# A gated short convolution beside a long one: the gate's product leaves PSUM early, and the long convolution's steps get lower rates

## The chip, the cores and the metric

The kernel runs on one core of a Trainium2 chip. The metric is the device time of one execution in microseconds (us), as the median of several runs. One core has a matrix engine (TensorE, PE in the profile), a vector engine (VectorE, DVE), an activation engine (ScalarE, ACT), a general engine (GpSimd, POOL) and DMA queues (SP). TensorE writes its products to PSUM banks; the other engines read them from there.

## What is computed

One inference step of a two-layer encoder over 1088 columns (1024 of a new stream and 64 of a running one), 1024 channels wide. The change lies in layer 1, whose mixer runs a long gated convolution C and a short gated convolution D from one normalised input:

```python
def odd_mixer(h, hist_c, hist_d, w_in, w_out, c_conv_w, c_conv_b, c_ln_g, c_ln_b, d_conv_w):
    z = h @ w_in
    c_in = z[..., :C_WIDTH] * jax.nn.sigmoid(z[..., C_WIDTH:2 * C_WIDTH])
    c_ext = jnp.concatenate([hist_c.astype(z.dtype), c_in], axis=1)
    c = causal_dwconv(c_ext, c_conv_w) + c_conv_b            # width 31
    c = jax.nn.silu(layer_norm(c, c_ln_g, c_ln_b))
    o = 2 * C_WIDTH
    gate_b = z[..., o:o + D_WIDTH]
    gate_c = z[..., o + D_WIDTH:o + 2 * D_WIDTH]
    xt = z[..., o + 2 * D_WIDTH:]
    d_ext = jnp.concatenate([hist_d.astype(z.dtype), gate_c * xt], axis=1)
    d = gate_b * causal_dwconv(d_ext, d_conv_w)              # width 3
    y = jnp.concatenate([c, d], axis=-1) @ w_out
    return y, c_ext[:, -(C_KERNEL - 1):], d_ext[:, -(D_KERNEL - 1):]
```

`rms_norm` comes before it and a feed-forward block with squared ReLU after it; both layers have that block, and it takes most of the time.

## The kernel before

Data lie with channels on the 128 partitions and the columns along the free axis. Each operand of a matrix product is kept as a high and a low part (`split`: the activation engine makes the high part, line 176, the vector engine the low part, line 177), and each product is three matmuls (`mm3`, lines 268 to 270).

In layer 1 the 512 channels of each of C and D are four groups j of 128. Every projection of a group (`project`) is made in two halves of 544 columns, the right one (c=1) first. A half is a PSUM pair of two banks that takes 48 matmuls. There are two such pairs (`open_psum("m1", 2)`), used in turn, so TensorE can start a half only when the vector engine has emptied the pair of the half before the last. Three more banks (`psum3`) hold the running sum of the long convolution.

First come the projections of C, two for each group (`cg`, `ca`, in `conv_pairs`). Its width-31 convolution is 31 steps for each group. Those of groups 1 and 3 and the last 13 of group 2 run on the vector engine, each as one multiply-and-add over 1118 columns in PSUM (`on_vec`, line 1131; the last step of a group is line 1137, and in group 2 line 1142 adds GpSimd's part). That makes 75 steps, of which the first of each group is made by the activation engine (line 1110). Group 0 and the first 18 steps of group 2 run as a multiply on the activation engine (line 1118) and an add on GpSimd (line 1120).

These steps are not emitted group after group. They wait in two lists, and `some(rates)` takes from them after each half: the rate is added to a credit, and each whole unit of it takes one step. A step for GpSimd is tied behind the last instruction of the activation engine that was emitted before it (`issue_after`). Behind the 75 steps the vector list holds 21 steps of C's layer norm (`ln_steps`: sums on GpSimd, `centre` with a matmul on line 1209, `scale` with one on line 1222, `finish_`), in three chunks of columns.

Then `short_conv(j)` runs for each group. It makes three projections: `dc`, whose halves leave PSUM into a buffer `wide` (line 1158); `dx`, whose halves are multiplied with that buffer into `z` (line 1162); and `db`, the gate. Between `dx` and `db` the width-3 convolution makes `o` from `z` (the activation engine on line 1171, the vector engine twice on line 1173, for a piece of 1024 and one of 64 columns). For a half of `db` the vector engine multiplies `o` by the norm's factor (line 1180) and then by the PSUM pair (line 1181), which only then is free, and `split` makes `dd`.

After that comes the output product of D (key `o1d`): sixteen halves of 24 matmuls, each added to `x` on line 766. Then that of C (`o1c`), first for all of the left half of the columns, which needs the first two chunks of the layer norm.

The order of the instructions on an engine is not the order of the text. A list planner in the language puts every traced instruction in order by its own costs, and an instruction that stands later in the text may be put ahead of one that is not yet ready. On the chip each engine then runs its list in order.

Of the kernel before, what the change touches and what calls it, by code (L numbers as in the profile page):

```python
# [13 lines left out]
AF = mybir.ActivationFunctionType  # L14
ALU = mybir.AluOpType
# [5 lines left out]
T = SEQ + DEC  # L21
# [5 lines left out]
NH = 2 * NQ  # L27
C4 = [(NQ * i, NQ * i + NQ) for i in range(4)]
CW = 512
HB, HC, HD = 15, 30, 2  # L30
# [13 lines left out]
def segs(a, b, halo):  # L44

    out = []
    if a < SEQ:
        e = min(b, SEQ)
        out.append((0, halo + a, e - a))
    if b > SEQ:  # L50
        s = max(a, SEQ)
        out.append((s - a, 2 * halo + s, b - s))
    return out
# [3 lines left out]
def encoder(ctx, tc, ins, outs):  # L57
    nc = tc.nc
    act, dve, gp, pe, dma = nc.scalar, nc.vector, nc.gpsimd, nc.tensor, nc.sync
# [30 lines left out]
    def sb(shape, dt, tag, bufs):  # L90
        uid[0] += 1
        p = opened["right"][1] if tag in RIGHT else opened["left"][1] if tag in LEFT else pool
        return p.tile(shape, dt, tag=tag, bufs=bufs, name=f"{tag}_{uid[0]}")
# [48 lines left out]
    def xs(n=T, dt=F32):  # L142
        return sb([P, n], dt, "X", 8)
# [27 lines left out]
    def col(o):  # L171
        return par[:, o : o + 1]


    def split(hi, lo, src):
        act.activation(hi, src, AF.Copy)  # L176
        dve.tensor_tensor(lo, src, hi.bitcast(F32), ALU.subtract)  # L177
# [76 lines left out]
    def take(key, depth=4):  # L254
        while key not in made:
            n = len(made)
            ahead(sum(s for s, _ in made.values()) + 2)
            assert len(made) > n, key
        got = made.pop(key)[1]
        ahead(depth)  # L260
        return got
# [69 lines left out]
    def halves(t):  # L331
        return t.rearrange("p (h t) -> p h t", h=2)
# [416 lines left out]
    def add_out(m, c, w, t, ks):  # L749
        a = c * NH  # L750
        ps = pair()
        for i in range(2):
            mm3(
                ps[:, i, :NQ],
                [
                    (
                        w[0][:, q * P : (q + 1) * P],
                        w[1][:, q * P : (q + 1) * P],
                        t(0, k, c, i),
                        t(1, k, c, i),  # L760
                    )
                    for q, k in ks
                ],
            )
        xm = halves(x[m][:, a : a + NH])
        dve.tensor_tensor(xm, xm, ps[:, :, :NQ], ALU.add)
# [220 lines left out]


    h = h1
    RP, RD, NP2 = (2.85, 1.65), (2.4, 1.65), 18  # L990
    NC = 2 * HC + T
    ND = 2 * HD + T
    NO = HC + T
# [6 lines left out]
    dd = [tuple(sb([P, T], F32R, "dd", 8) for _ in range(2)) for _ in range(4)]  # L1000
    wide = lambda: sb([P, NH], F32, "wide", 5)
# [7 lines left out]
    def last_on_act():  # L1009
        return next(i for i in reversed(nc.cur_bb.bb.instructions) if i.engine == mybir.EngineType.Activation)  # L1010

    def some(*rates):
        for i, q in enumerate((on_dve, on_pool)):
            credit[i] += rates[i]
            while credit[i] >= 1:
                credit[i] -= 1
                if q:
                    with tc.issue_after(last_on_act()) if q is on_pool else nullcontext():
                        q.pop(0)()

    def r_of(c):
        return halves(acc[:, c * NH : c * NH + NH])
# [3 lines left out]
    def project(key, ps_of, rates):  # L1026

        w = take(key)
        for c in (1, 0):
            ps = pair()  # L1030
            for i in range(2):
                a = i * NQ
                mm3(
                    ps[:, i, :NQ],
                    [
                        (
                            w[0][:, k * P : (k + 1) * P],
                            w[1][:, k * P : (k + 1) * P],
                            h[c][0][k][:, a : a + NQ],
                            h[c][1][k][:, a : a + NQ],  # L1040
                        )
                        for k in MS
                    ],
                )
            if unnormed:
                assert unnormed.pop(0) == c
                rms_half(c, wide(), psum3().rearrange("p (h t) -> p h t", h=3)[:, :2])
                rr = halves(r2[:, c * NH : c * NH + NH])
                dve.tensor_tensor(rr, r_of(c), r_of(c), ALU.mult)
            ps_of(c, ps[:, :, :NQ])  # L1050
            some(*rates)

    def pieces(c, t, ps, g, halo):

        g = halves(g)
        if c == 0:
            return [(halves(t[:, halo : halo + NH]), ps, g)]
        out = []
        for i in range(2):
            for s, o, n in segs(NH + i * NQ, NH + i * NQ + NQ, halo):  # L1060
                out.append((t[:, o : o + n], ps[:, i, s : s + n], g[:, i, s : s + n]))
        return out
# [87 lines left out]
    def short_conv(j):  # L1150
        gc = [None] * 2
        z, o = xs(ND), xs()
        dve.memset(z[:, :HD], 0.0)
        dma.dma_start(out=z[:, HD + SEQ : 2 * HD + SEQ], in_=ins["sdT"][j])

        def gate_c(c, ps):
            gc[c] = wide()
            dve.tensor_tensor(halves(gc[c]), ps, halves(r2[:, c * NH : c * NH + NH]), ALU.mult)

        def gate_x(c, ps):  # L1160
            for o_, p, g in pieces(c, z, ps, gc[c], HD):
                dve.tensor_tensor(o_, p, g, ALU.mult)

        project(("dc", j), gate_c, RD)
        project(("dx", j), gate_x, RD)
        dma.dma_start(out=outs["cd_p"][j], in_=z[:, SEQ : SEQ + HD])
        dma.dma_start(out=outs["cd_s"][j], in_=z[:, ND - HD :])
        wk = lambda k: col(O_DW + 3 * j + k)
        for s, e, n in segs(0, T, HD):
            e -= HD  # L1170
            act.activation(o[:, s : s + n], z[:, e : e + n], AF.Copy, scale=wk(0))
            for k in (1, 2):
                dve.scalar_tensor_tensor(  # L1173
                    out=o[:, s : s + n], in0=z[:, e + k : e + k + n], scalar=wk(k), in1=o[:, s : s + n],
                    op0=ALU.mult, op1=ALU.add,
                )
        def gate_b(c, ps):
            a = c * NH
            oc = o[:, a : a + NH]
            dve.tensor_tensor(halves(oc), halves(oc), r_of(c), ALU.mult)  # L1180
            dve.tensor_tensor(halves(oc), halves(oc), ps, ALU.mult)  # L1181
            split(dd[j][0][:, a : a + NH], dd[j][1][:, a : a + NH], oc)

        project(("db", j), gate_b, RD)

    means = {}
# [50 lines left out]
    for j in range(4):  # L1237
        short_conv(j)
# [4 lines left out]
    for m in MS:  # L1243
        w = take(("o1d", m))
        for c in range(2):
            add_out(m, c, w, dh, [(k, k) for k in range(4)])
            some(1.5, 0)
    while on_dve or on_pool:
        some(1, 1)
    open_psum("f1", 4)  # L1250
# [133 lines left out]
```

## Time and profile before

| | us |
|---|---|
| median of 3 runs | 2098.84 (2098.55 to 2103.15) |
| the profiled execution's own time | 2099.91 |
| its span in the profile | 2098.1 |

The profiled execution is 1.07 us above the median. Its span leaves 1.8 us around it. Times in the rows are microseconds from the span's start unless marked ns; "x48" is a number of instructions; a bracket at the end of a row says how long the engine stood idle before it and whose end let it go on.

### The profile page before, as it was taken

Reading aid. Unit: us, or ns where it says so; the run is one execution under the profiler, and the core shown is the slowest. Engines: PE = TensorE matmul, PEld = TensorE weight load, DVE = VectorE, ACT = ScalarE, POOL = GpSimd, SP = SyncE. Lnnn points to the kernel's source line nnn. Section 1 sums busy time; section 2 is a strip of 40 time slices with the busy share of each in tenths; the row PEclk is TensorE's granted clock in tenths of the full one; section 3 lists DMA queues with packets and bytes.
Section 4 is the critical chain, followed back from the end, with each engine's and each line's share of the span. In section 5 each row is a group of like instructions: output and inputs, shape, how many; then the busy total and the mean of one; then the engine's idle time right before and its main releaser. Section 6 shows DMA issues by size and latency. Waiting matters only on the chain.

```text
span 2098.1 us, 38092 instructions
## 1 busy us (share of the span) xinstructions
PE 2006.6 (96%) x15212; PEld 1974.7 (94%) x15212; DVE 1630.4 (78%) x2697; ACT 948.0 (45%) x1710; POOL 261.7 (12%) x172
## 2 busy tenths in 40 slices
PE   7999989999998999998999999989999999999995
PEld 5799989999998999998999999989999999999994
DVE  7884787676779888878499967897676779888867
ACT  6233554444445444445453425654344455444443
POOL 5200220000000000002276730210000000000003
PEclk9999999999999999999999999999999999999997
DMA  4223213434348444422211132223434366545402
GB/s 153 73 62 104 81 65 142 162 126 162 127 155 264 149 136 152 137 83 100 74 42 41 41 70 87 91 78 137 152 135 153 134 215 198 153 134 154 131 32 85
DMA packets 120434, 250.36 MB, mean 119 GB/s; under 512 B 16384, under 2 KB 31360, under 8 KB 116160
## 3 DMA queue, kind: packets, MB, share of 16 engines
q1 hardware_dynamic: 120256, 247.93, 36.3%
q8 instruction: 119, 1.95, 0.4%
q14 instruction: 59, 0.48, 0.1%
HBM read 176.26 MB, written 71.63 MB: 118 GB/s over the span
## 4 chain that ended last, share of the span: by engine, by line
PE 74%; DVE 17%; issue 2%; ACT 2%; POOL 2%; DMA 2%; DVEq 0%; SPq 0%; ACTq 0%; POOLq 0%
PE pp L861 20%; PE pp L863 20%; PE pp L862 19%; DVE ps L1131 4%; PE pp L268 3%; PE pp L269 3%; PE pp L270 3%; PE ps L268 2%; PE ps L269 2%; PE ps L270 2%; DVE Q L177 1%; DVE Wl L177 1%; DVE W L177 1%; DVE X L940 1%; DVE X L1173 1%
## 5 line engine op out<-in xcount | busy, mean ns | idle before, releaser
L861 PE MATMUL pp<-FA,W 128*128 128x272 f32 x1792 | 522.7, 293 | 36.5 <-DVE X L940 25.9
L861 PE MATMUL pp<-Q,W 128*128 128x272 f32 x1792 | 518.7, 290 | 2.0 <-DVE Q L903 1.1
L863 PE MATMUL pp<-FA,W 128*128 128x272 f32 x1792 | 520.1, 290 | 0.0
L862 PE MATMUL pp<-FA,W 128*128 128x272 f32 x1792 | 519.0, 290 | 0.0
L862 PE MATMUL pp<-Q,W 128*128 128x272 f32 x1792 | 516.9, 289 | 1.0 <-DVE Q L177 1.0
L863 PE MATMUL pp<-Q,W 128*128 128x272 f32 x1792 | 517.1, 289 | 0.0
L861 PEld LDWEIGHTS pp<-FA,W 128*128 128x128 f32 x1792 | 340.1, 190 | 43.2 <-DVE X L940 30.5
L862 PEld LDWEIGHTS pp<-FA,W 128*128 128x128 f32 x1792 | 342.7, 191 | 0.2
L862 PEld LDWEIGHTS pp<-Q,W 128*128 128x128 f32 x1792 | 340.3, 190 | 1.5 <-DVE Q L177 1.4
L861 PEld LDWEIGHTS pp<-Q,W 128*128 128x128 f32 x1792 | 338.9, 189 | 2.9 <-DVE X L940 1.4
L863 PEld LDWEIGHTS pp<-FA,W 128*128 128x128 f32 x1792 | 341.0, 190 | 0.0
L863 PEld LDWEIGHTS pp<-Q,W 128*128 128x128 f32 x1792 | 339.1, 189 | 0.0
L176 ACT ACTIVATE W<-RAW 128x512 fp32r<-128x512 f32 (+3 forms) x308 | 182.4, 595 | 150.5 <-PE pp L863 108.5
L177 DVE TENSOR_TENSOR W<-RAW,W 128x512 fp32r<-128x512 f32 (+3 forms) x308 | 204.7, 666 | 56.5 <-ACT W L176 55.7
L268 PE MATMUL pp<-Q,Wl 128*128 128x272 f32 x768 | 226.1, 294 | 12.8 <-DVE X L1181 10.4
L940 DVE TENSOR_TENSOR X<-X,pp 128x544 f32<-128x544 f32 (+1 forms) x280 | 191.7, 691 | 57.1 <-PE pp L863 54.4
L269 PE MATMUL pp<-Q,Wh 128*128 128x272 f32 x768 | 224.7, 293 | 0.0
L270 PE MATMUL pp<-Q,Wh 128*128 128x272 f32 x768 | 224.0, 292 | 0.0
L950 POOL TENSOR_TENSOR acc<-acc,sq 128x544 f32<-128x544 f32 (+1 forms) x24 | 29.7, 1236 | 1345.4 <-ACT sq L949 1344.8
L176 ACT ACTIVATE W<-e 128x512 fp32r<-128x512 f32 (+3 forms) x210 | 124.6, 593 | 158.6 <-PE pp L863 127.4
L177 DVE TENSOR_TENSOR W<-e,W 128x512 fp32r<-128x512 f32 (+3 forms) x210 | 136.9, 652 | 66.5 <-ACT W L176 66.2
L268 PEld LDWEIGHTS pp<-Q,Wl 128*128 128x128 f32 x768 | 147.9, 193 | 14.6 <-DVE X L1181 11.0
(220 smaller groups left out, 3541.7 us busy)
## 6 DMA issues: line engine op xcount, KB each, us to landing
RAW<-in_wf SPq DMA_DIRECT2D x58, 1024.0 KB, 5.2
vr<-hd SPq DMA_DIRECT2D x119, 272.0 KB, 2.8
hd<-Q SPq DMA_DIRECT2D x112, 272.0 KB, 2.3
Q<-hd SPq DMA_DIRECT2D x105, 272.0 KB, 2.8
hd<-vr SPq DMA_DIRECT2D x98, 272.0 KB, 2.2
raw<-in_wi SPq DMA_DIRECT2D x18, 512.0 KB, 3.4
X<-in_xT SPq DMA_DIRECT2D x8, 544.0 KB, 4.1
xd<-X SPq DMA_DIRECT2D x8, 544.0 KB, 2.7
```

Of the source, the lines that this page charges most:

```text
L176: act.activation(hi, src, AF.Copy)
L177: dve.tensor_tensor(lo, src, hi.bitcast(F32), ALU.subtract)
L268: pe.matmul(ps, ll, rh, start=s, stop=False)
L269: pe.matmul(ps, lh, rl, start=False, stop=False)
L270: pe.matmul(ps, lh, rh, start=False, stop=e)
L861: pe.matmul(ps, ll, hi, start=bool(s), stop=False, skip_group_check=True)
L862: pe.matmul(ps, lh, lo, start=False, stop=False, skip_group_check=True)
L863: pe.matmul(ps, lh, hi, start=False, stop=e, skip_group_check=True)
L940: dve.tensor_tensor(t, t, ps, ALU.subtract if f in (1, 4, 6) else ALU.add)
L950: (dve if j == 3 else gp).tensor_tensor(at, at, sq, ALU.add)
L1131: return dve.scalar_tensor_tensor(out=o, in0=z[:, k : k + NO], scalar=wk(k), in1=o, op0=ALU.mult, op1=ALU.add)
L1173: dve.scalar_tensor_tensor(out=o[:, s : s + n], in0=z[:, e + k : e + k + n], scalar=wk(k), in1=o[:, s : s + n], op0=ALU.mult, op1=ALU.add,)
```

## The change

The gate's half is multiplied by the norm's factor out of PSUM into a `wide` buffer, and the pair is free after that one instruction. The width-3 convolution is emitted after the first half's instruction. After the second half's, both halves of `o` are multiplied by their buffers, the right one first, and split. The vector rate in D's stage goes from 2.4 to 1.9 steps for each half, and in the output product of D from 1.5 to 2.

```diff
-    RP, RD, NP2 = (2.85, 1.65), (2.4, 1.65), 18
+    RP, RD, NP2 = (2.85, 1.65), (1.9, 1.65), 18
...
-        for s, e, n in segs(0, T, HD):
-            e -= HD
-            act.activation(o[:, s : s + n], z[:, e : e + n], AF.Copy, scale=wk(0))
-            for k in (1, 2):
-                dve.scalar_tensor_tensor(
-                    out=o[:, s : s + n], in0=z[:, e + k : e + k + n], scalar=wk(k), in1=o[:, s : s + n],
-                    op0=ALU.mult, op1=ALU.add,
-                )
+
+        def convolve():
+            for s, e, n in segs(0, T, HD):
+                e -= HD
+                act.activation(o[:, s : s + n], z[:, e : e + n], AF.Copy, scale=wk(0))
+                for k in (1, 2):
+                    dve.scalar_tensor_tensor(
+                        out=o[:, s : s + n], in0=z[:, e + k : e + k + n], scalar=wk(k), in1=o[:, s : s + n],
+                        op0=ALU.mult, op1=ALU.add,
+                    )
+
+        gb = {}
+
         def gate_b(c, ps):
-            a = c * NH
-            oc = o[:, a : a + NH]
-            dve.tensor_tensor(halves(oc), halves(oc), r_of(c), ALU.mult)
-            dve.tensor_tensor(halves(oc), halves(oc), ps, ALU.mult)
-            split(dd[j][0][:, a : a + NH], dd[j][1][:, a : a + NH], oc)
+
+            gb[c] = wide()
+            dve.tensor_tensor(halves(gb[c]), ps, r_of(c), ALU.mult)
+            if c == 1:
+                return convolve()
+            for i in (1, 0):
+                a = i * NH
+                oc = o[:, a : a + NH]
+                dve.tensor_tensor(oc, oc, gb[i], ALU.mult)
+                split(dd[j][0][:, a : a + NH], dd[j][1][:, a : a + NH], oc)
...
             add_out(m, c, w, dh, [(k, k) for k in range(4)])
-            some(1.5, 0)
+            some(2, 0)
```

## Rows read from the trace of the kernel before

**Rows 1.** The page: busy time, share of the span and instructions of each engine.
```profile
PE 2006.6 (96%) x15212; PEld 1974.7 (94%) x15212; DVE 1630.4 (78%) x2697; ACT 948.0 (45%) x1710; POOL 261.7 (12%) x172
```

**Rows 2.** The waits of TensorE, 1100 to 1265 us: total, times, longest.
```profile
PE pp L268 <- DVE X L1181: 10.4, 3, 4.3
```

**Rows 3.** Windows: length, busy time of each engine, granted clock, DMA share, GB/s.
```profile
1109.30:1231.30 122.00, 110.58 (x823) 109.02 (x822) 115.37 (x111) 48.87 (x49) 77.43 (x31) 0.94 0.13 36
1231.30:1261.30 30.00, 30.00 (x241) 30.00 (x240) 11.36 (x18) 4.36 (x7) 6.34 (x7) 1.00 0.56 137
1261.30:1315.20 53.90, 52.70 (x399) 50.52 (x398) 40.97 (x84) 30.66 (x58) 0.00 (x0) 1.00 0.20 66
```

**Rows 4.** The timeline of TensorE in D's stage: start, duration, instruction, idle before.
```profile
1110.07 0.39 PE L268 MATMUL pp<-Q,Wl 128*128 128x272 f32 x1 [0.17 <-DVE wide L1158]
...
1138.14 0.39 PE L268 MATMUL pp<-Q,Wl 128*128 128x272 f32 x1 [3.02 <-DVE X L1181]
...
1222.25 0.60 PE L268 MATMUL pp<-Q,Wl 128*128 128x272 f32 x1 [4.35 <-DVE X L1181]
```

**Rows 5.** The timeline of VectorE in D's stage: start, duration, instruction, idle before.
```profile
1114.30 1.39 DVE L1131 SCALAR_TENSOR_TENSOR ps<-cin,par,ps 128x1118 f32<-128x1118 f32 x1 [1.36 <-ACT ps L1110]
...
1128.08 0.71 DVE L1162 TENSOR_TENSOR X<-pp,wide 128x544 f32<-128x544 f32 x1
...
1137.37 0.71 DVE L1181 TENSOR_TENSOR X<-X,pp 128x544 f32<-128x544 f32 x1
...
1228.84 1.23 DVE L1142 TENSOR_TENSOR cin<-cin,X 128x1024 f32<-128x1024 f32 x1 [1.44 <-POOL X L1120]
...
1231.28 0.72 DVE L1158 TENSOR_TENSOR wide<-pp,r 128x544 f32<-128x544 f32 x1
1237.29 0.72 DVE L1158 TENSOR_TENSOR wide<-pp,r 128x544 f32<-128x544 f32 x1 [5.29 <-PE pp L270]
...
1261.34 0.72 DVE L1181 TENSOR_TENSOR X<-X,pp 128x544 f32<-128x544 f32 x1 [3.84 <-PE pp L270]
```

**Rows 6.** Groups of VectorE by form, 1109 to 1232 us: count, busy us, mean ns.
```profile
L1131 DVE SCALAR_TENSOR_TENSOR ps<-cin,par,ps 128x1118 f32<-128x1118 f32 x42 | 57.9, 1380 | 1.8 <-ACT ps L1110 1.4
L177 DVE TENSOR_TENSOR Wl<-raw,Wh 128x1024 fp32r<-128x1024 f32 x9 | 18.2, 2021 | 0.0
L1173 DVE SCALAR_TENSOR_TENSOR X<-X,par,X 128x1024 f32<-128x1024 f32 x6 | 9.8, 1629 | 0.0
L1173 DVE SCALAR_TENSOR_TENSOR X<-X,par,X 128x64 f32<-128x64 f32 x6 | 7.4, 1238 | 0.0
L177 DVE TENSOR_TENSOR dd<-X,dd 128x544 fp32r<-128x544 f32 x6 | 5.6, 939 | 0.7 <-ACT dd L176 0.7
L1158 DVE TENSOR_TENSOR wide<-pp,r 128x544 f32<-128x544 f32 x7 | 5.0, 720 | 2.5 <-PE pp L270 2.5
L1181 DVE TENSOR_TENSOR X<-X,pp 128x544 f32<-128x544 f32 x6 | 4.3, 714 | 0.0
L1180 DVE TENSOR_TENSOR X<-X,acc 128x544 f32<-128x544 f32 x6 | 4.1, 716 | 0.0
```

**Rows 7.** The timeline of GpSimd: the first adds after one of its pauses.
```profile
1140.05 11.90 POOL L1120 TENSOR_TENSOR X<-X,X 128x1118 f32<-128x1118 f32 x4 [14.75 <-ACT X L1118]
```

**Rows 8.** The timeline of VectorE at moments when GpSimd pauses: three two-input instructions.
```profile
1126.59 0.27 DVE L1173 SCALAR_TENSOR_TENSOR X<-X,par,X 128x64 f32<-128x64 f32 x1
...
1131.13 1.27 DVE L1173 SCALAR_TENSOR_TENSOR X<-X,par,X 128x1024 f32<-128x1024 f32 x1
...
1224.19 1.22 DVE L177 TENSOR_TENSOR Wl<-raw,Wh 128x1024 fp32r<-128x1024 f32 x1
```

**Rows 9.** The timeline from the layer norm's first matmul to D's last output half.
```profile
1261.14 0.77 PE L1209 MATMUL ps<-t,onec 128*128 128x364 f32 x2
...
1292.42 1.12 DVE L177 TENSOR_TENSOR Q<-cin,Q 128x180 fp32r<-128x180 f32 x4
...
1315.18 0.72 DVE L766 TENSOR_TENSOR X<-X,pp 128x544 f32<-128x544 f32 x1 [2.29 <-PE pp L270]
```

## The prediction

> **What bounds the kernel now.** I read the page first: TensorE is busy for 96% of the span, VectorE for 78% [rows 1], so the kernel is TensorE's except where something starves it. The waits of TensorE in D's stage name one cause: three waits, 10.4 us, for line 1181, the instruction that frees the gate's PSUM pair [rows 2]. The reader should see in the windows that from 1109.3 to 1231.3 VectorE works 115.4 of 122.0 us while TensorE's granted clock averages 0.94, and that in the next 30 us VectorE works only 11.4 and TensorE never stops [rows 3]. So the work of VectorE is crowded into the first three groups and missing in the fourth.
>
> What TensorE loses follows from its pace. In the fourth group four halves leave PSUM in 1261.34 - 1237.29 = 24.05 us, 6.01 for each pair [rows 5]. From 1110.07, where the third half of the stage starts [rows 4], to 1261.34, where the last one is complete [rows 5], lie 22 pairs, 132.3 us at that pace; it took 151.3. The loss is **19.0 us**, and no change inside this stage can give more. Of it 10.4 are the waits on line 1181, and the clock, partly at its lower level of 1.2 GHz, costs (1 - 0.94) x 122 = 7.3. The rest is short waits.
>
> How late line 1181 is: the second half of `dx` is taken at 1128.08, and the first half of the gate only at 1137.37, 9.3 us later [rows 5]. In between stand a weight split, conv steps, the width-3 convolution and two multiplications by the norm's factor.
>
> **The change part by part.**
>
> *The gate's product.* Before, a half of the gate costs two multiplications, 0.716 from SBUF alone and 0.714 with PSUM; after, one from PSUM into a buffer, for which line 1158 with the same operands stands at 0.720, and one from SBUF alone, 0.716 as line 1180 [rows 6]. The work is the same; what changes is that the pair is free after the first of the two, and the convolution and its products no longer stand before it. The three waits, 3.02 and 4.35 among them [rows 4], go. Behind the waiting instruction on VectorE stood conv steps, which nobody was waiting for. The buffers: four of five `wide` tiles are in use in a group, so I price this wait at nothing; a half's lateness, 6.0, is the price if one were missing. The state's two DMAs stay where they were, ahead of the convolution.
>
> *But is the waiting replaced by VectorE's own load?* From the first eviction of the first group to that of the fourth, VectorE has 115.4 us of work [rows 3], TensorE 18 pairs, 18 x 6.01 = 108.2. VectorE is the slower one. A reordering alone leaves 115.4 to be done before the fourth group. Of its 6.6 us of idleness there, 1.36 (a group's first step on the activation engine) and 1.44 (GpSimd's part of group 2) stay [rows 5]; the rest is mostly waiting for a TensorE that had itself been held (2.5 before line 1158 [rows 6]) and goes.
>
> *The lower rates.* At 2.4, 18 halves of this stage after the 22.8 steps of C's stage make 66 of the 75 conv steps due by 1231. Yet all 75 are done there: 42 of line 1131 lie in that stretch [rows 6], line 1142, which ends the last group, is at 1228.84 [rows 5]. So the steps run nine ahead of what the rates ask, that is, they fill any gap in which nothing of earlier text is ready. A rate that is not the limit can be lowered without moving anything: at 1.9 they would merely be 18 ahead. I take zero. If the rate did bind, nine of the steps would leave the stretch, 9 x 1.38 = 12.4 us [rows 6].
>
> *GpSimd against VectorE.* Instructions of VectorE with two SBUF inputs are sometimes much longer: the 64-column piece of line 1173 takes 0.27 and the 1024-column piece 1.27 when GpSimd pauses, a weight split 1.22 [rows 8]; in the stretch the means are 1.238, 1.629 and 2.021 [rows 6], while line 1131, with one input in PSUM, has a mean of 1.380 [rows 6] and 1.39 in the row shown [rows 5]. The excess is 6 x 0.97 + 6 x 0.36 + 9 x 0.80 + 6 x 0.22 (the split of `dd`, 0.939 against 0.72) = 16.5 us. Line 1180 has none, since GpSimd stands still there: 14.75 us, because its next multiply is tied behind the split of `dd` [rows 7]. After, it is tied behind the width-3 convolution and starts sooner, so the new products and the four free 1024-column pieces can be held. Below, this is worth down to -16.5 (nothing held any more); above, ten instructions at the 0.97 of the worst group, +9.7. I take the nearest rows in size: 6 x 0.22 as for `dd`, 4 x 0.36 as for the group's mean, **+2.7**, because the number of GpSimd's adds is unchanged and what meets one here no longer meets it elsewhere.
>
> The Trainium skill, SBUF — State Buffer, section "Who interferes with whom", says that such a VectorE instruction and a GpSimd one that reads SBUF exclude each other for the whole of the instruction. The lengthening in the rows agrees. Taken by itself it speaks against this change, and the second rival below is what it would do.
>
> *The sum.* The fourth group's first eviction: 1109.3 + 115.4 + 2.8 + 2.7 = 1230.2, against 1231.28 [rows 5]. But before, TensorE then had five pairs to do, as it had been stopped before it could fill the second; now it stands with both full, and four remain after the 0.72 of the eviction: 1230.2 + 0.72 + 24.05 = 1255.0 against 1261.34, **6.4 gained**. At the end the second half of `dd` in the fourth group comes after one product more than before: 0.7 lost, for the output product waits for it. The layer norm's steps fall due later, but TensorE has 53.9 us there (next part); zero. The remaining kernel shifts. So 5.7 us: 2099.91 - 5.7 = 2094.2 on the profiled execution, and, since that one is 1.07 above the median, **2093** for the median. What a measurement of this kernel tells from no change is 0.3%, 6.3 us; the forecast lies just inside it.
>
> **The rivals.**
>
> *The rates bind after all.* Then VectorE has 115.4 - 12.4 = 103.0 against 108.2, TensorE never waits, and the whole 19.0 less 0.7 comes back; the moved steps fit into the 18.6 idle microseconds of the fourth group [rows 3]. 2099.91 - 18.3 - 1.07 = 2080.5. Against it stand the nine steps ahead. Chance 0.20.
>
> *GpSimd's hold eats it.* With +9.7 for +2.7 the sum becomes -1.3 (gain 5.7 - 7.0), that is 2100 for the median. For it: the pause at line 1180 that goes [rows 7]. Against: GpSimd's 77.4 us [rows 3] are not more than before. Chance 0.13. This is also the case of a change that does what it says and shows nothing.
>
> *The norm becomes late.* The side of slower. With 1.9 and 2 the norm's first matmul (step 79 of the list) is due in the sixth half of D's output product, (79 - 68.4) / 2 = 5.3, not at its start; half a pair each, 3.0 us, makes it 18 us later. From that matmul to the last split that the left half of C's output product needs, 1261.14 to 1293.54, it takes 32.4; 18 + 32.4 = 50.4, and D's output product lasts 1315.18 - 1261.34 = 53.8 [rows 9]. So 3.4 are to spare, and each microsecond more is paid on TensorE. It decides from a slip of 3.4 + 5.7 + 6.3 = 15.4 us, if the norm's steps, now in between sixteen evictions, take half as long again; for that price, 8 to 10 us lost, the median would be 2107. Chance 0.07.
>
> **How the numbers follow.** The forecast case has 0.60, with its own range 2089 to 2097: 0.27 of it lies beyond 0.3% faster, 0.33 within. With the first rival (0.20 faster), the second (0.11 same, 0.02 slower) and the third (0.06 slower, 0.01 same): faster 0.47, same 0.45, slower 0.08. The range is 2081 to 2100: the first rival's neighbourhood and the second's, without the third.
>
> **What would show it.** Right: no wait of TensorE on the gate's product above 1 us; instead short waits spread over the evictions, at full clock; VectorE still over 95% busy until the fourth group; the last conv step still before the fourth group's first eviction; that eviction within 2 us of 1230, and D's output product starting about 6 us earlier. Wrong: conv steps in the fourth group or in D's output product (first rival); line 1173 or the products at 2 us and more throughout (second); TensorE waiting at the start of C's output product (third). What most endangers the forecast is the claim that the order ignores the rates: with it falls the size, not the sign.

## The result, and the profile after

| | before | after |
|---|---|---|
| median of 5 runs, us | 2101.61 | 2087.64 |
| ratio, 95% interval | 1 | 0.9948 (0.9936 to 0.9960) |
| the profiled execution's span, us | 2098.1 | 2085.8 |

The kernel became 0.5% faster: about 11 us, with an interval of 8 to 13, where 5.7 had been forecast. The median before had been 2098.84 in the three runs shown ahead of the prediction and is 2101.61 in these five, so the ratio, and not the difference of the two medians, is the size to use.

The windows of the same three stretches: D's first three groups, the fourth group, D's output product (columns as in [rows 3]).

```profile
1110.08:1226.20 116.12, 110.28 (x861) 108.25 (x861) 109.80 (x110) 48.69 (x49) 78.34 (x30) 1.00 0.13 37
1226.20:1251.47 25.27, 25.27 (x204) 25.27 (x203) 12.62 (x19) 4.37 (x7) 8.36 (x8) 1.00 0.67 165
1251.47:1303.57 52.10, 52.10 (x398) 50.51 (x397) 42.13 (x84) 30.45 (x56) 0.00 (x0) 1.00 0.21 67
```

The first stretch fell from 122.0 to 116.1 us, the second from 30.0 to 25.3, the third from 53.9 to 52.1; that is 12.4 of the span's 12.3. The granted clock of the first stretch is 1.00, where it was 0.94: TensorE ran at 2.4 GHz throughout. VectorE works 109.8 us in it instead of 115.4, with as many instructions within one or two.

The waits of TensorE, 1090 to 1330 us (total, times, longest), against [rows 2]:

```profile
PE pp L268 <- DVE X L1162: 3.6, 3, 1.4
PE pp L268 <- DVE wide L1185: 2.0, 2, 1.5
PE pp L268 <- DVE wide L1158: 0.2, 1, 0.2
```

Line 1185 is the gate's new eviction (the instruction that empties the PSUM pair). What had been three waits of 3 to 4.3 us on one instruction are six of 1.5 us at most, on all three evictions: TensorE still waits for VectorE, by less.

The timeline of VectorE, to be read against [rows 5]:

```profile
1134.40 0.71 DVE L1185 TENSOR_TENSOR wide<-pp,acc 128x544 f32<-128x544 f32 x1
...
1188.40 2.81 DVE L1131 SCALAR_TENSOR_TENSOR ps<-cin,par,ps 128x1118 f32<-128x1118 f32 x2 [2.20 <-ACT ps L1110]
...
1224.86 1.22 DVE L1142 TENSOR_TENSOR cin<-cin,X 128x1024 f32<-128x1024 f32 x1 [1.46 <-POOL X L1120]
1226.01 0.27 DVE L1137 SCALAR_TENSOR_TENSOR cin<-cin,par,ps 128x64 f32<-128x64 f32 x1
1226.20 0.72 DVE L1158 TENSOR_TENSOR wide<-pp,r 128x544 f32<-128x544 f32 x1
```

The gate's first half leaves PSUM 5.5 us after the last half of `dx` (1128.86), not 9.3. The last group's conv steps still end right at the fourth group's first eviction: the lower rate took none of them out of the first three groups.

The groups of VectorE by form, 1110 to 1227 us, against [rows 6]:

```profile
L1131 DVE SCALAR_TENSOR_TENSOR ps<-cin,par,ps 128x1118 f32<-128x1118 f32 x42 | 57.9, 1379 | 4.0 <-ACT ps L1110 3.6
L177 DVE TENSOR_TENSOR Wl<-raw,Wh 128x1024 fp32r<-128x1024 f32 x9 | 12.7, 1409 | 0.0
L1175 DVE SCALAR_TENSOR_TENSOR X<-X,par,X 128x1024 f32<-128x1024 f32 x6 | 9.6, 1595 | 0.0
L1191 DVE TENSOR_TENSOR X<-X,wide 128x544 f32<-128x544 f32 x6 | 7.0, 1170 | 0.0
L1175 DVE SCALAR_TENSOR_TENSOR X<-X,par,X 128x64 f32<-128x64 f32 x6 | 7.0, 1163 | 0.0
...
L177 DVE TENSOR_TENSOR dd<-X,dd 128x544 fp32r<-128x544 f32 x6 | 4.3, 715 | 0.7 <-ACT dd L176 0.7
```

The 42 conv steps are as many and as long as before. The new product (line 1191) is held, 1.170 where line 1180 took 0.716: 2.7 us more. But the nine weight splits went from 2.021 to 1.409, 5.5 us less, and the splits of `dd` from 0.939 to 0.715, 1.3 less. GpSimd's timeline fits that:

```profile
1132.02 7.20 POOL L1120 TENSOR_TENSOR X<-X,X 128x1118 f32<-128x1118 f32 x2 [5.94 <-ACT X L1118]
1146.08 5.33 POOL L1120 TENSOR_TENSOR X<-X,X 128x1118 f32<-128x1118 f32 x2 [6.87 <-ACT X L1118]
...
1182.96 22.26 POOL L1120 TENSOR_TENSOR X<-X,X 128x1118 f32<-128x1118 f32 x8 [5.74 <-ACT X L1118]
```

The pause of 14.75 us [rows 7] is now two short ones with adds between them. In the kernel before the adds came in a burst after the pause, from 1140.05 on, and the next group's weight split fell into it:

```profile
1145.87 3.62 DVE L177 TENSOR_TENSOR Wl<-raw,Wh 128x1024 fp32r<-128x1024 f32 x1
```

Of the nine weight splits five took more than 1.3 us in the kernel before, each beside an add of GpSimd. After the change one does (2.98 us, inside the run of eight adds above).

### The profile page after: what moved, and what is told of

Its sections match the earlier page's. It is cut to its first block, busy times and chain, and to the rows that moved or that the text cites. A ratio compares the mean times of both kernels' runs of the same rounds, so it can differ in the third digit from the quotient of the medians.

```text
span 2085.8 us, 38083 instructions
## 1 busy us (share of the span) xinstructions
PE 1997.7 (96%) x15212; PEld 1965.2 (94%) x15212; DVE 1627.1 (78%) x2697; ACT 949.0 (45%) x1710; POOL 264.7 (13%) x172
## 4 chain that ended last, share of the span: by engine, by line
PE 73%; DVE 17%; ACT 3%; issue 3%; DMA 2%; POOL 2%; SPq 0%; DVEq 0%; ACTq 0%; POOLq 0%
PE pp L861 19%; PE pp L863 19%; PE pp L862 19%; DVE ps L1131 4%; PE pp L268 3%; PE pp L269 3%; PE pp L270 3%; PE ps L268 2%; PE ps L270 2%; PE ps L269 2%; DVE Q L177 1%; DVE W L177 1%; DVE X L940 1%; DVE Wl L177 1%; DMA vr<-hd 1%
## 5 line engine op out<-in xcount | busy, mean ns | idle before, releaser
L176 ACT ACTIVATE W<-RAW 128x512 fp32r<-128x512 f32 (+3 forms) x308 | 182.3, 595 | 141.4 <-PE pp L863 107.5
L269 PE MATMUL pp<-Q,Wh 128*128 128x272 f32 x768 | 221.6, 289 | 0.0
L270 PE MATMUL pp<-Q,Wh 128*128 128x272 f32 x768 | 220.9, 288 | 0.0
```

What stands on the lines that cost most here:

```text
L269: pe.matmul(ps, lh, rl, start=False, stop=False)
L270: pe.matmul(ps, lh, rh, start=False, stop=e)
```

## The experiments

Two theories were open. The first, of the prediction: the early release does it, and the lower rates move nothing. The second: the rates take load off VectorE. A third came out of the profile above: what counts is when GpSimd's adds run. Executions differ by a few microseconds ahead of layer 1's mixer, so the table counts from the first start of the norm's factor there (line 1049 in the kernel before) to D's last eviction and to the last addition of D's output product (line 766), in the profiled execution. TensorE does the same in the first 100 us after that start in all thirteen profiles, 98.63 us of work and one wait of 1.4, so what a kernel gains up to D's end it gains on D. The first eviction of D falls anywhere from 94.7 to 100.1 us after the norm, by how far VectorE lags; the expectations mostly count D's stage from there, and the column "first to last" has that length. The ratio is to the kernel before, measured beside each.

| kernel | norm | D's last eviction | product's last addition | to D's end | to product's end | first to last | ratio, 95% interval |
|---|---|---|---|---|---|---|---|
| before | 1009.19 | 1261.34 | 1315.18 | 252.2 | 306.0 | 152.0 | 1 |
| after | 1009.99 | 1251.47 | 1303.57 | 241.5 | 293.6 | 141.4 | 0.9948 (0.9936 to 0.9960) |
| e1_gate_only | 1009.88 | 1251.36 | 1305.27 | 241.5 | 295.4 | 141.4 | 0.9945 (0.9931 to 0.9959) |
| e2_rates_only | 1010.53 | 1258.88 | 1311.94 | 248.4 | 301.4 | 148.3 | 0.9962 (0.9949 to 0.9975) |
| e7_evict_alone | 1008.14 | 1258.30 | 1310.41 | 250.2 | 302.3 | 150.0 | 0.9978 (0.9967 to 0.9989) |
| e8_tie_alone | 1011.17 | 1261.72 | 1315.64 | 250.6 | 304.5 | 150.5 | 1.0000 (0.9988 to 1.0011) |
| e5_before_no_adds | 1014.77 | 1247.80 | 1301.54 | 233.0 | 286.8 | 138.1 | 0.9916 (0.9902 to 0.9929) |
| e6_after_no_adds | 1009.68 | 1242.70 | 1295.21 | 233.0 | 285.5 | 138.1 | 0.9910 (0.9897 to 0.9924) |
| e3_tied | 1015.21 | 1248.33 | 1307.03 | 233.1 | 291.8 | 134.3 | 0.9949 (0.9933 to 0.9965) |
| e4_tied_old_gate | 1011.74 | 1245.95 | 1304.11 | 234.2 | 292.4 | 135.4 | 0.9941 (0.9920 to 0.9961) |
| e9_tied_in_d | 1009.43 | 1251.03 | 1305.12 | 241.6 | 295.7 | 146.9 | 0.9955 (0.9943 to 0.9968) |
| e11_tied_21 | 1012.75 | 1248.68 | 1307.84 | 235.9 | 295.1 | 137.1 | 0.9954 (0.9935 to 0.9972) |
| e12_tied_22 | 1006.82 | 1246.41 | 1306.55 | 239.6 | 299.7 | 140.8 | 0.9973 (0.9962 to 0.9984) |

**The gate alone.** The changed kernel with the old rates:

```diff
-    RP, RD, NP2 = (2.85, 1.65), (1.9, 1.65), 18
+    RP, RD, NP2 = (2.85, 1.65), (2.4, 1.65), 18
...
-            some(2, 0)
+            some(1.5, 0)
```

> The new gate with the old rates (2.4 and 1.5). Order theory (the early release of the gate's pair does it, the rates move no conv step): D's stage, first to last eviction, stays at the 141 us of the changed kernel against 152 before, all conv steps again end before the fourth group, and only the layer norm starts early again, so that D's output product takes 53.8 instead of 52.1 us; in all about 10 us faster than before, ratio 0.995 to 0.996. Rate theory (the lower rates take load off VectorE): D's stage goes back to 146 us or more, and the gain is at most half, ratio 0.997 or above.

D's stage is the changed kernel's to a tenth of a microsecond, its VectorE works the same 109.8 us, and the output product takes 53.9 us instead of 52.1. With the new gate the rates are worth those 1.8 us: the layer norm's first matmul comes 15.1 us after D's last eviction instead of just before it, and the short waits that TensorE has in this output product, 1.3 us in all, are not there in the changed kernel's. By time the two kernels can't be told apart. The rate theory falls as an account of D's stage.

**The rates alone.** The kernel before with 1.9 and 2.

> The old gate with the new rates (1.9 and 2). Order theory: the three waits of TensorE on line 1181, 10.4 us, are all there, D's stage stays within 2 us of 152; D's output product shortens to about 52 us; in all 0 to 3 us faster than before, ratio 0.9985 to 1.000. Rate theory: the waits shrink to under 5 us and the gain is 6 us or more, ratio 0.997 or below.

A miss: 5 to 11 us faster by the ratio, 4.6 by the trace, 3.8 of it in D's stage. The three waits on line 1181 are there as expected (9.3 us), and 42 conv steps lie in the first three groups as before. But VectorE works 110.6 us there, 4.7 less than before, while it works 3.7 more in the fourth group (15.1 for 11.4): line 1142, which ends the last group's convolution, now comes behind the first eviction. And the weight split that took 3.62 us in the kernel before stands three conv steps earlier, in a pause of GpSimd, and takes 1.22.

```profile
1143.98 1.22 DVE L177 TENSOR_TENSOR Wl<-raw,Wh 128x1024 fp32r<-128x1024 f32 x1
```

So the rates do touch D's stage, though no conv step of line 1131 left the stretch: a few instructions changed places. GpSimd's first long pause also went here (5.94 and 6.36 us in place of 14.75), with its tie as before. That the planner's new order did both is likely; by what steps was not followed.

**The early release alone.** In the changed kernel, lower rates included, the convolution is emitted before the gate's projection again, and each half is finished after its own eviction:

```diff
             dve.tensor_tensor(halves(gb[c]), ps, r_of(c), ALU.mult)
-            if c == 1:
-                return convolve()
-            for i in (1, 0):
-                a = i * NH
-                oc = o[:, a : a + NH]
-                dve.tensor_tensor(oc, oc, gb[i], ALU.mult)
-                split(dd[j][0][:, a : a + NH], dd[j][1][:, a : a + NH], oc)
+            a = c * NH
+            oc = o[:, a : a + NH]
+            dve.tensor_tensor(oc, oc, gb[c], ALU.mult)
+            split(dd[j][0][:, a : a + NH], dd[j][1][:, a : a + NH], oc)
+
+        convolve()
```

> The changed kernel, but the width-3 convolution is emitted before the gate's projection again and each half is multiplied and split right after its own eviction. The pair is still free after one instruction, but GpSimd's next add is again tied behind the split of dd. If only the early release counts: within 2 us of the changed kernel. If it counts that GpSimd no longer pauses and then works while the weight splits run: VectorE's work in the first three groups goes back from 109.8 towards 115 us, the weight splits from 1.41 towards 2.0 us each, and the time is 4 to 6 us above the changed kernel's.

D's stage gains 2.0 us of the change's 10.7. Against the rates-only run, which has the same rates and the old gate, it is 1.8 us longer to D's end. The pair does leave early: in the first three groups its first half is taken 7.8, 6.7 and 6.7 us after the last half of `dx`, where it was 9.3, 9.3 and 13.3. But GpSimd pauses 11.4 and 14.0 us in the second and third group, VectorE's work is above that of the kernel before, and TensorE now waits for VectorE at the next eviction, line 1158. This is the second view, with a larger loss: 8.7 us more than the changed kernel to the product's end. The window of the first three groups, two groups of VectorE in it, and that wait:

```profile
1108.25:1230.46 122.21, 112.69 (x869) 110.61 (x867) 118.37 (x108) 50.27 (x51) 77.28 (x29) 0.99 0.12 36
```

```profile
L177 DVE TENSOR_TENSOR Wl<-raw,Wh 128x1024 fp32r<-128x1024 f32 x9 | 18.2, 2017 | 0.0
L177 DVE TENSOR_TENSOR dd<-X,dd 128x544 fp32r<-128x544 f32 x6 | 9.1, 1515 | 0.7 <-ACT dd L176 0.7
```

```profile
PE pp L268 <- DVE wide L1158: 6.6, 3, 3.2
```

**GpSimd's tie alone.** The kernel before, with its step after the gate's first half tied as in the changed kernel:

```diff
-                    with tc.issue_after(last_on_act()) if q is on_pool else nullcontext():
+                    with tc.issue_after(anchor[-1] if anchor else last_on_act()) if q is on_pool else nullcontext():
...
+        width3 = last_on_act()
+
         def gate_b(c, ps):
+            anchor[:] = [width3] if c == 1 else []
```

> The kernel before, gate and rates untouched, but GpSimd's step after the gate's first half is tied behind the width-3 convolution's multiply, as it is in the changed kernel, and no longer behind the split of dd. Tie theory (the early release alone won 2 us in D's stage; what the change mostly did is to let GpSimd's adds run during the pause, so that they no longer meet the weight splits): GpSimd's pauses of 14.7 us shrink below 8, the weight splits go from 2.02 to about 1.4 us each, VectorE's work in the first three groups falls from 115 to 111 or less, and D's stage from 152 to 144 to 148; 4 to 8 us faster than before. Release theory (the pair's early release is what counts, and the other run was slow for its order of the products): line 1181 is as late as before, D's stage 150 to 152, 0 to 2 us faster.

The pauses are short (7.4 us at most), the weight splits take 1.375, VectorE's work is 113.1 us; and the time is unchanged. The tie theory of this expectation missed: 4 to 8 us had been forecast by it. TensorE's waits on the gate's second product (line 1185 in this text) are all there:

```profile
PE pp L268 <- DVE X L1185: 10.9, 3, 5.1
```

The adds now run where the convolution and the products by the norm's factor stand, and hold those: the products take 1.251 for 0.716, and the pair leaves 11.4 to 11.5 us after `dx` in the first three groups.

So neither half of the change does much by itself, 2.0 and 1.6 us in D's stage, and the two together 10.7. With the early release alone VectorE sets the pace, with more work than before. With the tie alone VectorE has less, and waits for a TensorE that stands at the late pair. The two runs do not split the change cleanly: the changed kernel differs from the first not only by the tie but also by the place of the convolution and of the products behind the evictions, and the release with the tie and the old places was not run.

**Without GpSimd's adds.** In the kernel before and in the changed one the adds of the long convolution on GpSimd are left out, but for the last of a group, so the sums of groups 0 and 2 lack most of their terms:

```diff
             if k < 30:
-                return gp.tensor_tensor(o, o, t, ALU.add)
+                return
```

> The kernel before with GpSimd's adds of the long convolution left out (but the last of each group), so that the sums of groups 0 and 2 lack most terms; the multiplies on the activation engine stay. If GpSimd's hold is what makes VectorE the slower engine: no instruction with two SBUF inputs is lengthened (weight splits 1.22, 64-column pieces 0.28), VectorE's work in the first three groups falls from 115 to about 100 us, under TensorE's 108, the waits on line 1181 go below 3 us in all, D's stage takes 133 to 137 us: 13 to 19 us faster. If VectorE's own load does it: work of 110 us or more and D's stage above 145.

> The changed kernel with the same adds of GpSimd left out. If the early release of the pair matters by itself, D's stage is shorter than in the kernel before without the adds by 2 us or more. If the two are the same within 1.5 us in D's stage (133 to 136 us both), then the change was worth what it took out of the meeting of GpSimd and VectorE, and the late release alone costs nothing while VectorE keeps up.

The kernel before without the adds, the window of the first three groups and the groups of VectorE in it:

```profile
1109.70:1217.94 108.24, 108.24 (x867) 108.24 (x866) 99.50 (x110) 49.05 (x49) 4.94 (x5) 1.00 0.14 40
```

```profile
L1131 DVE SCALAR_TENSOR_TENSOR ps<-cin,par,ps 128x1118 f32<-128x1118 f32 x42 | 58.0, 1382 | 3.5 <-ACT ps L1110 3.2
L177 DVE TENSOR_TENSOR Wl<-raw,Wh 128x1024 fp32r<-128x1024 f32 x9 | 11.0, 1220 | 0.4
L1173 DVE SCALAR_TENSOR_TENSOR X<-X,par,X 128x1024 f32<-128x1024 f32 x6 | 7.7, 1279 | 0.0
...
L1173 DVE SCALAR_TENSOR_TENSOR X<-X,par,X 128x64 f32<-128x64 f32 x6 | 1.7, 278 | 0.0
```

Every lengthening is gone, and VectorE's work is 99.5 us, 15.9 less than in [rows 3]. TensorE never stops. The old gate still stands behind the convolution, 9.5 us after `dx` was taken (1127.54 to 1137.05), and TensorE has no wait for it. In the changed kernel without the adds the pair leaves 5.5 to 6.7 us after `dx`, and the same window has the same pace:

```profile
1104.60:1212.64 108.04, 108.04 (x865) 108.04 (x864) 99.06 (x110) 49.52 (x49) 3.68 (x4) 1.00 0.14 40
```

To D's end both kernels take 233.0 us, and 138.1 from D's first eviction to its last: **the early release is worth nothing here while VectorE keeps up.** The Trainium skill, SBUF — State Buffer, section "Who interferes with whom", says that a VectorE instruction with two SBUF inputs contends with a GpSimd one that reads SBUF, and that one with at most one SBUF input, outside the modes that use two ports, does not. The traces agree in both directions: without the adds the instructions with two SBUF inputs fall to their shortest, and line 1131, with one, stays at 1.38.

**The rates made to bind.** In the changed kernel each step of VectorE's list is tied behind the last VectorE instruction emitted before it:

```diff
...
-                    with tc.issue_after(last_on_act()) if q is on_pool else nullcontext():
+                    with tc.issue_after(last_on(mybir.EngineType.Activation if q is on_pool else mybir.EngineType.DVE)):
```

> The changed kernel with each step of VectorE's list tied behind the last VectorE instruction emitted before it, as GpSimd's already are, so that the rates 1.9 and 2 do set the order. If VectorE's load in the first three groups is what still costs TensorE there: conv steps in the fourth group and in D's output product, no wait of TensorE in D's stage above 0.5 us, D's stage at 133 to 135 us instead of 141, and some of that (2 to 5 us) given back in D's output product, where conv steps and the layer norm now both stand: 2 to 6 us faster than the changed kernel. If what costs is GpSimd holding VectorE, wherever the steps stand: no gain, or the loss in the output product alone, 0 to 5 us slower.

The three windows:

```profile
1114.03:1220.97 106.94, 106.94 (x856) 106.94 (x855) 99.68 (x95) 48.19 (x48) 78.41 (x29) 1.00 0.14 41
1220.97:1248.33 27.36, 27.36 (x221) 27.36 (x220) 21.82 (x28) 5.56 (x8) 0.18 (x1) 1.00 0.62 136
1248.33:1307.03 58.70, 53.93 (x405) 51.45 (x404) 53.44 (x93) 30.17 (x54) 8.08 (x8) 1.00 0.19 59
```

Here the rates do what their name says: 33 conv steps in the first three groups instead of 42, the others in the fourth, where VectorE now works 21.8 us, and in the output product. D's stage runs at TensorE's pace and ends 8.4 us earlier than in the changed kernel. The output product gives 6.6 of them back; the conv steps and the layer norm now meet in it, and VectorE works 53.4 us there instead of 42.1. By time nothing is won, where 2 to 6 us had been expected.

The same ties and rates with the old gate:

> The old gate with the rates 1.9 and 2 and VectorE's steps tied everywhere, so that the rates set the order: the run with the changed gate and these ties, but for the gate. If a late release costs only where VectorE is behind: D's stage ends as early as with the changed gate (within 1.5 us, counted from the first projection's norm), no wait of TensorE on line 1181 above 1 us, and the time is that run's, ratio 0.994 to 0.996. If the early release is needed as such: waits on line 1181 of 5 us and more, D's stage 5 us or more longer.

D's end at 234.2 against 233.1 and the same time within the intervals, as the first view had it. This run can't confirm that a late release is free, however, for with the ties the new gate does not release the pair much earlier: 6.8, 8.6, 8.2 and 6.9 us after `dx` in the four groups, against 8.1, 8.0, 8.6 and 8.1 with the old one. For that there is only the pair of runs without the adds.

**Versions between.** The tie in D's stage alone with the old rates; and ties everywhere with 2.1 and 2.5, and with 2.2 and 2.

> The changed gate with the old rates, 2.4 and 1.5, and VectorE's steps tied as in the run where the rates set the order, but in D's stage alone: C's stage stays as it is, the conv steps end in the fourth group, and the layer norm starts with D's output product. D's stage 133 to 136 us instead of 141, first eviction of D no later than in the changed kernel, D's output product 53 to 55 us: 4 to 8 us faster than the changed kernel, 0.991 to 0.993 of the kernel before. If the tie costs as much as it saves here too: within 2 us of the changed kernel.

> The changed gate, steps tied everywhere, rates 2.1 in D's stage and 2.5 in its output product, so that 73 of the 75 conv steps are due by the end of D and the norm starts earlier. If the 8 us that the tie saves in D were lost again only to conv steps standing in the output product: D's stage as short as with 1.9, its output product 54 to 56 us instead of 58.7, 3 to 5 us faster than the changed kernel. If VectorE is behind again as soon as more steps stand in D: D's stage longer by 4 us or more, no gain over the changed kernel.

> The same with 2.2 and 2: all conv steps due in D. First view: D's stage 1 to 3 us longer than with 1.9, output product 54 us, 2 to 5 us faster than the changed kernel. Second view: D's stage longer by 6 us or more, within 2 us of the changed kernel or slower.

None is faster than the changed kernel, and the last is slower than it by the ratios. With 2.4 tied, D ends no earlier at all (241.6 against 241.5): VectorE works 113.2 us in the first three groups although 39 conv steps lie there, because the 64-column pieces take 1.787 and the 1024-column ones 1.967. Its output product takes 54.1 us, as expected. With 2.1 and 2.2 D's stage is 2.8 and 6.5 us longer than with 1.9, and the output product takes 59.2 and 60.1 us against 58.7: the first view of both runs was wrong on the product, which did not shorten although fewer conv steps stand in it. Why was not settled. No version that beats both kernels was found.

## Why the prediction came out as it did

The direction of the forecast held, and much of its mechanism: the sign, the range (2081 to 2100), the end of the three waits, the conv steps that stay, TensorE at full clock with short waits. Three of its own signs were missed. The longest wait on the gate's product is 1.5 us and not under 1, VectorE is busy 94.6% of the first three groups and not over 95, and the fourth group's first eviction is at 1226.2, not within 2 us of 1230. The gain was twice the forecast, so that the median lies below the forecast case's own range (2089 to 2097). By its terms, for the first eviction of the fourth group counted from that of the first:

| term | forecast, us | measured, us |
|---|---|---|
| VectorE's work before the change | 115.4 | 115.4 |
| GpSimd against VectorE | +2.7 | -5.6 (109.8 of work) |
| idleness that stays | 2.8 | 6.3 (116.1 - 109.8; 3.6 at line 1110, 1.46 at GpSimd) |
| together | 120.9 | 116.1 |
| to D's last eviction | 24.8 | 25.3 |
| D's stage | 145.7 | 141.4 |
| D's output product, against before | +0.7 | -1.7 |

*The term that failed is the hold by GpSimd*, +2.7 with bounds of -16.5 and +9.7. It was argued that what meets one add no longer meets another, so the sum would grow only by the new products and the four 1024-column pieces that had been free. The products grew from 4.1 to 7.0 us, twice the 1.3 priced for them; the 1024-column pieces, priced at 1.4 more, went from 9.8 to 9.6. That the two come near 2.7 together is luck. And which instructions the adds meet is not a matter of their number: in a burst after a pause they met the weight splits, 1.2 us long and held to 3.6; in shorter runs they met one of the nine. Conv steps, which have one input in SBUF, took 1.38 with and without the adds, so in these traces an add that meets only those costs VectorE nothing. The run with the release alone shows the other sign, work up by 3.0 to 118.4, with the burst kept. The earlier tie of GpSimd's steps, which the prediction had priced as a cost, is the likely reason that the burst went, and without that the release gave little.

*The idleness* was under-priced by 3.5: the first step of the last group on the activation engine cost a second wait of 2.20. The two errors partly cancel.

*TensorE two pairs ahead* held in substance: it does not wait after the fourth group's first eviction, and D ends 25.3 us after it where the forecast had 24.8.

*The end of D and the layer norm:* the forecast was a loss of 0.7; the late norm was a gain of 1.8 instead (the changed kernel against the gate-alone run). The third rival, a norm that comes too late, did not come: its first matmul is 15.1 us after D's last eviction, where 18 had been forecast, and TensorE has no wait at the start of C's output product.

*"The lower rates move nothing"* was right for this change in D's stage, to a tenth of a microsecond, and wrong as a general statement: with the old gate the same numbers were worth 3.8 us there, by instructions that changed places.

*The first rival* (the rates bind) did not happen here; made to happen by ties, it gave 19.1 us up to D's end against the kernel before (252.2 to 233.1), as its ceiling of 19.0 had it, and lost most of the difference in the next stage. *The second* (GpSimd's hold eats the gain) was about the right mechanism with the wrong sign.

## What to carry to other kernels

A buffer that is freed late cost nothing here by itself; it cost when the engine that frees it was also behind. Before moving the release, compare that engine's work in the stage with the pace of the engine that waits, and find what lengthens its instructions. Where VectorE and GpSimd share a stage, look at which two-input instructions meet GpSimd's adds: running the same adds at another moment took 5.6 us of work off VectorE here, and neither that nor the early release did much without the other. A lower rate in the text spread nothing here, since the planner fills every gap anyway; only a tie made it bind, and then the load appeared in the next stage.

## What was unexpected of the hardware

In the kernel before, a VectorE instruction of 1.22 us with two SBUF inputs took up to 3.62 us next to GpSimd's adds of some 2.8, three times its length, and a 64-column one of 0.28 up to 1.84; without the adds both were at their shortest each time. The whole of it was 15.9 us of VectorE's work in 122. TensorE's waits of up to 1.5 us left its granted clock at 1.00 over the stretch, where three of 3.0 to 4.3 us had gone with 0.94. In the run with 2.4 tied, two waits of at most 1.8 us went with 0.97.
